# Hybrid encoder layer on one core: the first stage's TensorE order, the places of the next rows' squares, and the turning of the weights' rows

## The chip, the cores and the metric

The kernel runs on one core of one Trainium2 chip. Its engines run side by side and meet through semaphores: PE (TensorE: matrix products and transpositions), DVE (VectorE), ACT (ScalarE), POOL (GpSimd) and SP (SyncE, which here only issues DMAs). The metric is device time in microseconds (us), the median of several runs of the whole kernel.

## The reference, cut to what matters

One encoder layer over 2048 rows of width 1024, all in float32. A conditioning vector c gives six modulation vectors; the rows are normalised, modulated and projected, then go through windowed attention and a bidirectional mLSTM, an output projection, and a gated feed-forward part.

```python
mod = jax.nn.silu(c) @ w_mod + b_mod
shift1, scale1, gate1, shift2, scale2, gate2 = jnp.split(mod, 6, axis=-1)
hmix = rms_norm(x, g_norm1) * (1.0 + scale1) + shift1
q_a, k_a, v_a, q_m, k_m, v_m, o_m, gates = jnp.split(hmix @ w_in, IN_SPLITS, axis=-1)
att = rms_norm(banded_attention(q_a, k_a, v_a, sink), g_attn_out)
qk = jax.nn.silu(centred_dwconv(concat([q_m, k_m]), conv_w, conv_b))
h_m = sigmoid(o_m) * rms_norm(mlstm_forward(qk, v_m, gates) + mlstm_backward(qk, v_m, gates), g_mlstm_out)
x = x + gate1 * (concat([att, h_m]) @ w_out)
hff = rms_norm(x, g_norm2) * (1.0 + scale2) + shift2
gte, up = jnp.split(hff @ w_ffn_in, 2, axis=-1)
x = x + gate2 * ((jax.nn.silu(gte) * up) @ w_ffn_out)
return rms_norm(x, g_final)
```

The edit lies in what makes `hmix` and its first products, and in one store of `o_m`.

## The kernel before, in words

**Tiling.** The rows are 16 tiles of 128 (tt = 0 to 15), in four blocks of 512 (n = 0 to 3). `xts[n]` holds a block's four row tiles, `hT[n]` the normalised and modulated block turned, so that the 1024 columns lie on eight slices k of 128 partitions. Every float32 value goes into TensorE as a high and a low part: `mm3` (L55 to L58) makes a product of three matmuls, high by high, high by low, low by high.

**The first stage** (L282 to L570) does three things side by side. It loads x and the parts of w_mod for the first two modulations, shift (m = 0) and scale (m = 1), in two halves each (`wm`); the first halves come by `mod_sum`, the second ones by `part_sum` on DVE (eight sums over k into `acc[0]` for the scale, into `acc[1]` for the shift), `by_col` (TensorE adds over the partitions and puts the result in columns, bank d), `mod_bias` and `scales` (which makes `gs1`). It normalises: `squares` (ACT, the line of each is L167), `rsqrt` (twelve very small DVE instructions), `scaled`. And it turns the block and multiplies: for slice k `trn(k)` transposes four 128 by 128 pieces on TensorE into PSUM bank b (k even) or d (k odd), `turn(k)` takes them out on ACT with scale and shift (L429) and rounds the high part (L430), `low(k)` makes the low part on DVE (L434), and `prods(k, tiles)` multiplies slice k of some of tiles 0 to 2 by the columns of w_in for values and gates (`nat_mm`: 272 columns into `pa`, 384 into `pv`). Tiles 0 to 2 hold six banks for their sums until slices 6 and 7 are added in the loop below; `nat_hi`, `small_lo` and `nat_lo` split the weights.

**The tile loop** (L525 to L568) goes over blocks and tiles. While block n is multiplied, `norm1(n + 1)` prepares the next one: its first step is squares, rsqrt and scaled; each further step turns one slice (`turned_split`: TensorE L182, ACT L183, DVE L189 and L190). `EVERY` says after how many products a step comes: every second one in tile 3, every eighth in tiles 4 to 7. After a tile its sums are taken out (L559 to L563: `vs` and `va`; `vs` has a single buffer) and stored (L567, L568). `columns_of(1, ...)` turns 48 rows of small weights (norm gains, convolution) into columns with one transposition into bank d and a DVE copy; it stands ahead of tile 4. `mod_row(2)` computes the gate row of the third modulation: loads (L375), sums on DVE (L379, L381), a split (L140, L141), and at the ends of tiles 5 and 6 two matmuls on TensorE (L387, L388).

**Order.** TensorE's order is that of the program in the whole kernel (`hand`). Up to `pre.close()` (L520) the orders of DVE, ACT, POOL and SP are also those of the program. Behind it these engines' instructions are put in order by a planner, by its own reckoning of costs; it may also put later instructions between earlier, fixed ones, as it does with the squares of the second and third block. Every engine and every DMA queue then works in order. The loads and stores of attention (`att_loads`, L842 to L846; the stores L907) go through SP's queue; the stores of `o_tiles` (L652, the gate rows og of the mLSTM heads) go through SP's queue too, but for two that go through ACT's. Their source tile has one buffer.

Of the kernel before, what the change touches and what calls it, by code (L numbers as in the profile page):

```python
# [11 lines left out]
F32 = mybir.dt.float32  # L12
F32R = mybir.dt.float32r
BF16 = mybir.dt.bfloat16
I32 = mybir.dt.int32
AF = mybir.ActivationFunctionType
# [20 lines left out]
def hybrid_layer_kernel(  # L37
# [53 lines left out]
    def rsqrt(pl, v, n, d, tag, bufs=2):  # L91

        vv, hh, yi, a = (pl.tile([P, n], dt, tag=tag + i, name=tag + i, bufs=bufs)
                         for i, dt in (("v", F32), ("h", F32), ("y", I32), ("a", F32)))
        y = yi.bitcast(F32)
        o = 0
        for v_, w, d_ in v if isinstance(v, list) else [(v, n, d)]:
            dve.tensor_scalar(vv[:, o:o + w], v_, 1.0 / d_, EPS, MUL, ADD)
            o += w
        dve.tensor_scalar(yi, vv.bitcast(I32), -0.5, 1597463007.0, MUL, ADD)  # L100
        dve.tensor_scalar(hh, vv, -0.5, None, MUL)
        for _ in range(3):
            dve.tensor_tensor(a, y, y, MUL)
            dve.tensor_tensor(a, a, hh, MUL)
            dve.scalar_tensor_tensor(y, a, 1.5, y, ADD, MUL)
        return y
# [55 lines left out]
    def squares(pl, xt):  # L162

        ssq = pl.tile([P, 4], F32, tag="ssq", name="ssq")
        for i in range(4):
            jk = pl.tile([P, D], BF16, tag="junk", name="junk", bufs=1)
            act.activation(jk, xt[i], AF.Square, accum_out=ssq[:, i:i + 1])  # L167
        return ssq

    def scaled(xt, r, on_act=False):  # L170

        for i in range(4):
            if on_act:
                act.activation(xt[i], xt[i], AF.Copy, scale=r[:, i:i + 1])
            else:
                dve.tensor_scalar(xt[i], xt[i], r[:, i:i + 1], None, MUL)
# [100 lines left out]
    with tc.tile_pool(name="sw", bufs=2, side="right", reuse_waits="tile") as sw:  # L277
# [29 lines left out]
        def columns_of(z, o, n):  # L307
            ps = bank("ad"[z], "colps")
            pe.transpose(ps[:, :n], rows[z], ident[:n, :n])
            dve.tensor_copy(cols[:, o:o + n], ps[:, :n])  # L310
# [32 lines left out]
        def nat_hi(z):  # L343
            act.activation(wh[:, BD[z], :144], wn[z][0], AF.Copy)
            for k in range(4 * z, 4 * z + 4):
                act.activation(wh[:, k, 144:], nat_part(k), AF.Copy)
# [5 lines left out]
        def nat_lo(k):  # L352
            dve.tensor_tensor(wl[:, k, 144:], nat_part(k), wh[:, k, 144:].bitcast(F32), SUB)

        def norm1(n, xt):
            hT.append(Kt(n, f"hT{n}"))
            scaled(xt, rsqrt(s1, squares(s1, xt), 4, D, "rs"))
            yield True
            for k in range(KT):
                turned_split(s1, xt, k, gs1, mod[:, 0, :], hT[n])  # L360
                yield True
# [60 lines left out]
        def trn(k):  # L422
            tps[k] = ps = bank("bd"[k % 2], "trn")
            for i in range(4):
                pe.transpose(ps[:, i * P:(i + 1) * P], x0[i][:, k * P:(k + 1) * P], ident)

        def turn(k):
            t = s1.tile([P, 512], F32, tag="ntmp", name="ntmp", bufs=2)
            act.activation(t, tps.pop(k), AF.Identity, bias=mod[:, 0, k:k + 1], scale=gs1[:, k:k + 1])  # L429
            act.activation(h0(0, k), t, AF.Copy)  # L430
            tps[k] = t

        def low(k):
            dve.tensor_tensor(h0(1, k), tps.pop(k), h0(0, k).bitcast(F32), SUB)  # L434

        def prods(k, tiles):
            for i in tiles:
                deque(nat_mm(0, i, *ops[i], (k,)), 0)

        def part_sum(acc, m, ks):  # L440
            for k in ks:
                w = wm[m, 1][k // 2][:, k % 2, :]
                if k == 0:
                    dve.tensor_scalar(acc, w, sc_col[:, k:k + 1], None, MUL)
                else:
                    dve.scalar_tensor_tensor(acc, w, sc_col[:, k:k + 1], acc, MUL, ADD)

        def by_col(acc):
            ps = bank("d", "modps")
            for k in range(4):  # L450
                pe.matmul(ps[:, k:k + 1], acc[:, k * P:(k + 1) * P], ones[:, 0:1], start=True, stop=True)
            return ps
# [21 lines left out]
        low(0)  # L474
        nat_lo(3)
        trn(2)
        prods(0, range(3))
        turn(1)
        low(1)
        part_sum(acc[0], 1, (0,))  # L480
        trn(3)
        prods(1, range(3))
        turn(2)
        low(2)
        part_sum(acc[0], 1, (1,))
        trn(4)
        prods(2, range(3))
        turn(3)
        low(3)
        part_sum(acc[0], 1, range(2, KT))  # L490
        nat_hi(1)
        ps = by_col(acc[0])
        part_sum(acc[1], 0, range(4))
        mod_bias(1, 1, ps)
# [11 lines left out]
        low(4)  # L506
        prods(4, (0,))
        trn(6)
        turn(5)
        nat_lo(6)  # L510
        low(5)
        prods(4, (1, 2))
        trn(7)
        turn(6)
        nat_lo(7)
        low(6)
        turn(7)
        low(7)
        prods(5, range(3))
        pre.close()  # L520
        gn = cp.tile([P, 2, 2, HM, NT], F32, name="gn")
        bgv = bg.rearrange("p (d y h) -> p y d h", d=2, y=2)
# [2 lines left out]
        for n in range(NB):  # L525
            if n + 1 < NB:
                nrm = norm1(n + 1, xts[n + 1])
                next(nrm)
            if n == 0:
                xts.append(load_x(3))  # L530
            if n == 1:
                vecs = mod_row(2)
                columns_of(1, N_A, N_B)
                dve.tensor_scalar(cvw, cols[:, O_CW:O_CW + 24].rearrange("p (j k) -> p j k", j=3), 0.5, None, MUL)
                dve.tensor_scalar(cvb, cols[:, O_CB:O_CB + KT], 0.5, None, MUL)
                dve.tensor_scalar(gml, cols[:, O_GM:O_GM + HM], 0.5, None, MUL)
            if n + 1 == NB:
                w_first = proj_cols(C_KM)
            for i in range(4):
                tt = 4 * n + i  # L540
                if tt < 3:
                    pa, pv = ops[i]
                else:
                    pa, pv = bank("g", "pa"), bank("a", "pv")
                ev = EVERY[n][i]
                for j, _ in enumerate(nat_mm(n, i, pa, pv, range(6 if tt < 3 else 0, KT))):
                    if ev and j % ev == ev - 1:
                        next(nrm, None)
                if tt == 8:
                    deque(nrm, 0)  # L550
                    wrow = deque(["w1h", "w1l", "wm0", "wm1"])
                    xs.close()
                    wp = ctx.enter_context(tc.tile_pool(name="w", bufs=1, side="left", reuse_waits="tile"))
                    wslots.extend([(wp, 0), (wp, 1)])
                    vecs = chain.from_iterable(mod_row(m) for m in (3, 4))
                vs = sw.tile([P, KV, 2, HD], F32R, tag="vs", name="vs", bufs=1)
                va = sw.tile([P, HM, 129], F32, tag="va", name="va")
                pav = pa[:, :128].rearrange("p (k d) -> p k d", k=KV)
                act.activation(vs[:, :, 0, :], pav, AF.Copy)  # L559
                dve.tensor_tensor(vs[:, :, 1, :], pav, vs[:, :, 0, :].bitcast(F32), SUB)  # L560
                dve.tensor_tensor(gn[:, :, :, :, tt], pa[:, 128:144].rearrange("p (d y h) -> p y d h", d=2, y=2), bgv, ADD)
                act.activation(va[:, 0, :128], pa[:, 144:272], AF.Copy)
                act.activation(va[:, 1:, :128], pv[:, :384].rearrange("p (h d) -> p h d", d=128), AF.Copy)  # L563
                pool.memset(va[:, :, 128:129], 1.0)
                if tt < 9 or tt % 2 == 0:
                    next(vecs, None)
                sp.dma_start(vst_d[tt * P:(tt + 1) * P], vs.bitcast(F32))  # L567
                sp.dma_start(vaug_d[tt * P:(tt + 1) * P], va)  # L568
# [71 lines left out]
    def o_tiles(heads, blocks, ws_):  # L640

        if not ws_:
            ws_.extend(proj_cols(C_OM + h * P) for h in heads)
        for n in blocks:
            for h, w in zip(heads, ws_):
                ps = bank("g", "gps")
                yield from proj_mm(ps, w, n)
                pl, tag = oslots[0]
                oslots.rotate(-1)
                t = pl.tile([P, 512], F32, tag=tag, name="oth", bufs=1)  # L650
                act.activation(t, ps, AF.Tanh, scale=0.5)
                (act if heads == (1,) and n < 2 else sp).dma_start(og_d[n, :, :, h], t.rearrange("p (c t) -> p c t", c=4))  # L652

    later = []

# [1436 lines left out]
```

## Time and profile before

| | |
|---|---|
| runs, median of 3 | 2260.43 us (2260.26 to 2260.79) |
| the profiled execution | 2263.72 us |
| its span, first to last instruction | 2261.9 us |
| mean granted TensorE clock | 0.992 |
| busy: PE, DVE, ACT, POOL | 2216.6 (98%), 1619.1 (72%), 1065.5 (47%), 1035.0 (46%) us |
| chain that ended last | PE 87%, DMA 4%, DVE 4%, ACT 2%, issue 1% |

How to read it: busy times count what an engine executes, not what it waits for. A timeline row gives start, time, engine, line, operation, out<-in, shapes and count, and in brackets the engine's idle time before it with what ended that time. A row of the waits gives who waited for whom, the total, the count and the longest. A row of windows gives the stretch and its length, then for PE, PE's weight loads, DVE, ACT and POOL the busy time with the number of instructions, then the granted clock, the share of the DMA engines and GB/s.

### The profile page before, as it was taken

The page shows a single profiled execution, that of the slowest core. Times are in us where ns is not written, and L with a number is a line of the kernel's source. Part 1 is how long each engine was busy: PE and PEld are TensorE (multiplying, and loading weights), DVE is VectorE, ACT ScalarE, POOL GpSimd, SP SyncE. Part 2 cuts the span into 40 slices and gives each one's busy share as a digit, 9 for nine tenths or more (in the row PEclk, how much of TensorE's full clock was granted, in tenths as well). Part 3 has the DMA queues.
Part 4 walks back from the last instruction along what each step waited for, and adds up shares of the span by engine and source line. Part 5 has one row for each costly group of instructions (what it writes and reads, how often), then busy time and mean ns, then how long its engine had stood idle before and what let it go on. Part 6 is the DMA issues. An engine that isn't in the chain of part 4 may idle for free.

```text
span 2261.9 us, 32339 instructions
## 1 busy us (share of the span) xinstructions
PE 2216.6 (98%) x10808; PEld 1861.0 (82%) x10808; DVE 1619.1 (72%) x2942; ACT 1065.5 (47%) x2216; POOL 1035.0 (46%) x900
## 2 busy tenths in 40 slices
PE   6999999999999999999999999999999999999998
PEld 5998888888788878888888888888888888888887
DVE  6766668656688877886767786777766665785694
ACT  5434565554578746354445434433333333233452
POOL 0016535434343333436666565467665664692020
PEclk8999999999999999999999999999999999999999
DMA  8566755685666575764343454534333374542462
GB/s 311 180 203 218 220 159 173 190 243 162 202 186 188 174 250 205 267 235 156 108 145 110 154 182 168 172 126 140 98 112 98 112 260 141 171 150 95 148 214 93
DMA packets 337063, 391.28 MB, mean 173 GB/s; under 512 B 20874, under 2 KB 234234, under 8 KB 336896
## 3 DMA queue, kind: packets, MB, share of 16 engines
q1 hardware_dynamic: 335616, 388.65, 52.7%
q8 instruction: 85, 1.39, 0.3%
q14 instruction: 82, 0.67, 0.1%
q10 hardware_dynamic: 1280, 0.56, 0.1%
HBM read 269.95 MB, written 119.19 MB: 172 GB/s over the span
## 4 chain that ended last, share of the span: by engine, by line
PE 87%; DMA 4%; DVE 4%; ACT 2%; issue 1%; SPq 0%; POOL 0%; ACTq 0%; POOLq 0%; DVEq 0%
PE gps L579 14%; PE fp L56 12%; PE fp L58 12%; PE fp L57 12%; PE fo L58 5%; PE fo L57 5%; PE fo L56 5%; PE ops L56 2%; PE ops L58 2%; PE ops L57 2%; PE atp L889 1%; PE num L790 1%; PE kvp L703 1%; PE num L792 1%; PE ao L902 1%
## 5 line engine op out<-in xcount | busy, mean ns | idle before, releaser
L579 PE MATMUL gps<-hT,whi 128*128 128x512 f32 x1088 | 395.7, 418 | 1.2 <-DVE cacc L594 1.2
L58 PE MATMUL fo<-w,al 128*128 128x512 f32 x616 | 239.8, 389 | 0.1
L57 PE MATMUL fo<-w,ah 128*128 128x512 f32 x616 | 239.7, 389 | 0.0
L56 PE MATMUL fo<-w,ah 128*128 128x512 f32 x616 | 239.7, 389 | 0.0
L579 PE MATMUL gps<-hT,wlo 128*128 128x512 f32 x544 | 226.3, 416 | 0.0
L579 PEld LDWEIGHTS gps<-hT,whi 128*128 128x128 f32 x1088 | 199.7, 190 | 25.1 <-DVE cacc L594 1.6
L56 PE MATMUL fp<-T,S 128*128 128x512 f32 x528 | 206.7, 391 | 0.0
L57 PE MATMUL fp<-T,S 128*128 128x512 f32 x528 | 205.7, 389 | 0.0
L58 PE MATMUL fp<-T,S 128*128 128x512 f32 x528 | 205.4, 389 | 0.0
L1846 DVE TENSOR_TENSOR al<-al,ah 128x1024 fp32r<-128x1024 f32 x77 | 116.2, 1514 | 105.7 <-ACT ah L1845 105.5
L1845 ACT ACTIVATE ah<-al 128x1024 fp32r<-128x1024 f32 x77 | 81.6, 1060 | 181.9 <-DMA al<-a_d 177.4
L1548 DVE TENSOR_TENSOR S<-sf,S 128x512 fp32r<-128x512 f32 x86 | 130.6, 1556 | 33.4 <-ACT S L1547 33.2
L1548 DVE TENSOR_TENSOR A<-graw,A 128x512 fp32r<-128x512 f32 x86 | 131.4, 1549 | 14.1 <-ACT A L1547 14.1
L58 PE MATMUL fp<-B,A 128*128 128x512 f32 x352 | 136.9, 389 | 0.0
L56 PE MATMUL fp<-B,A 128*128 128x512 f32 x352 | 136.9, 389 | 0.0
L57 PE MATMUL fp<-B,A 128*128 128x512 f32 x352 | 136.9, 389 | 0.0
L58 PEld LDWEIGHTS fo<-w,al 128*128 128x128 f32 x616 | 115.6, 188 | 24.5 <-DVE al L1846 0.6
L56 PEld LDWEIGHTS fo<-w,ah 128*128 128x128 f32 x616 | 115.6, 188 | 24.2
L57 PEld LDWEIGHTS fo<-w,ah 128*128 128x128 f32 x616 | 115.6, 188 | 24.0
L882 POOL TENSOR_SCALAR ap<-ap,adn 128x384 f32<-128x384 f32 (+1 forms) x124 | 70.2, 585 | 134.8 <-PE atp L889 62.3
L1715 DVE SCALAR_TENSOR_TENSOR g<-t,g 128x512 f32<-128x512 f32 x44 | 45.2, 1026 | 114.7 <-ACT t L1714 114.7
L1552 POOL TENSOR_TENSOR sf<-A,A22r 128x512 f32<-128x512 f32 x42 | 58.3, 1389 | 145.5 <-DMA A22r<-in_w_ffn_in_dram 121.7
(448 smaller groups left out, 6157.2 us busy)
## 6 DMA issues: line engine op xcount, KB each, us to landing
al<-a_d SPq DMA_DIRECT2D x77, 512.0 KB, 3.7
wmod<-in_w_mod_dram SPq DMA_DIRECT2D x48, 512.0 KB, 7.6
graw<-in_w_ffn_in_dram SPq DMA_DIRECT2D x43, 512.0 KB, 3.8
a_d<-ka SPq DMA_DIRECT2D x66, 256.0 KB, 4.8
bc<-bc_d SPq DMA_DIRECT2D x64, 256.0 KB, 4.6
hop_d<-n SPq DMA_DIRECT2D x56, 256.0 KB, 3.5
a_d<-u SPq DMA_DIRECT2D x55, 256.0 KB, 4.7
mqk<-qk_d SPq DMA_DIRECT2D x44, 256.0 KB, 4.6
```

Source lines behind the costliest of these rows:

```text
L56: pe.matmul(o, lh, rh, start=first, stop=False, skip_group_check=skip)
L57: pe.matmul(o, lh, rl, start=False, stop=False, skip_group_check=skip)
L58: pe.matmul(o, ll, rh, start=False, stop=last, skip_group_check=skip)
L579: pe.matmul(ps, w[i == 2][:, k, :], hT[n](i == 1, k), start=(k == 0 and i == 0), stop=(k == KT - 1 and i == 2))
L703: pe.matmul(kvp[:, :129], kn, vw, start=True, stop=True)
L790: pe.matmul(num[:, d, :129], sc[:, d, :], va_c, start=True, stop=st is None)
L882: pool.tensor_scalar(p, p, dn[:, g:g + 1], 0.0, MUL, ADD)
L1548: dve.tensor_tensor(t[:, 1, :], f, t[:, 0, :].bitcast(F32), SUB)
L1552: add.tensor_tensor(f1, a21, a22, ADD)
L1715: dve.scalar_tensor_tensor(g0, t0, 1.0, g0, ADD, MUL)
L1845: act.activation(ah, al.bitcast(F32), AF.Copy)
L1846: dve.tensor_tensor(al, al.bitcast(F32), ah.bitcast(F32), SUB)
```

## The change

`squares` is split so that one row tile's square can be placed alone. In the part with fixed orders, trn(3) moves from behind prods(0, tiles 0 to 2) to behind prods(0, tile 0); trn(4) from behind prods(1, tiles 0 to 2) to behind prods(1, tile 0); acc[0]'s third sum moves ahead of the fourth slice's low part. The second block's squares get places on ACT (three behind nat_hi(1), one ahead of turn(5)), its rsqrt and scaled get places on DVE (behind nat_lo(7), which moves ahead of turn(6), and behind low(7)); the third block's squares stand on ACT behind those. `norm1(1)` then has no first step left, and `norm1(2)` only rsqrt and scaled. `columns_of(1, ...)` and the three small scalings behind it move from ahead of tile 4 to ahead of tile 7. In `o_tiles` the two stores through ACT's queue are those of head 0 for blocks 2 and 3, no longer those of head 1 for blocks 0 and 1.

```diff
+    def square(pl, xt, i, ssq):
+        jk = pl.tile([P, D], BF16, tag="junk", name="junk", bufs=1)
+        act.activation(jk, xt[i], AF.Square, accum_out=ssq[:, i:i + 1])
...
         def norm1(n, xt):
             hT.append(Kt(n, f"hT{n}"))
-            scaled(xt, rsqrt(s1, squares(s1, xt), 4, D, "rs"))
+            if n > 1:
+                scaled(xt, rsqrt(s1, ssq2 if n == 2 else squares(s1, xt), 4, D, "rs"))
             yield True
...
         low(0)
         nat_lo(3)
         trn(2)
-        prods(0, range(3))
+        prods(0, (0,))
         turn(1)
         low(1)
         part_sum(acc[0], 1, (0,))
         trn(3)
-        prods(1, range(3))
+        prods(0, (1, 2))
         turn(2)
         low(2)
-        part_sum(acc[0], 1, (1,))
+        part_sum(acc[0], 1, (1, 2))
+        prods(1, (0,))
         trn(4)
-        prods(2, range(3))
+        prods(1, (1, 2))
         turn(3)
         low(3)
-        part_sum(acc[0], 1, range(2, KT))
+        part_sum(acc[0], 1, range(3, KT))
+        prods(2, range(3))
         nat_hi(1)
+        ssq1, ssq2 = (s1.tile([P, 4], F32, tag="ssq", name="ssq") for _ in range(2))
+        for i in range(3):
+            square(s1, xts[1], i, ssq1)
         ps = by_col(acc[0])
...
         trn(6)
+        square(s1, xts[1], 3, ssq1)
         turn(5)
         nat_lo(6)
         low(5)
         prods(4, (1, 2))
         trn(7)
+        nat_lo(7)
+        r1 = rsqrt(s1, ssq1, 4, D, "rs")
         turn(6)
-        nat_lo(7)
         low(6)
         turn(7)
         low(7)
+        scaled(xts[1], r1)
         prods(5, range(3))
+        for i in range(4):
+            square(s1, xts[2], i, ssq2)
         pre.close()
...
             if n == 1:
                 vecs = mod_row(2)
-                columns_of(1, N_A, N_B)
-                dve.tensor_scalar(cvw, cols[:, O_CW:O_CW + 24].rearrange("p (j k) -> p j k", j=3), 0.5, None, MUL)
-                dve.tensor_scalar(cvb, cols[:, O_CB:O_CB + KT], 0.5, None, MUL)
-                dve.tensor_scalar(gml, cols[:, O_GM:O_GM + HM], 0.5, None, MUL)
...
+                if tt == 7:
+                    columns_of(1, N_A, N_B)
+                    dve.tensor_scalar(cvw, cols[:, O_CW:O_CW + 24].rearrange("p (j k) -> p j k", j=3), 0.5, None, MUL)
+                    dve.tensor_scalar(cvb, cols[:, O_CB:O_CB + KT], 0.5, None, MUL)
+                    dve.tensor_scalar(gml, cols[:, O_GM:O_GM + HM], 0.5, None, MUL)
                 for j, _ in enumerate(nat_mm(n, i, pa, pv, range(6 if tt < 3 else 0, KT))):
...
-                (act if heads == (1,) and n < 2 else sp).dma_start(og_d[n, :, :, h], t.rearrange("p (c t) -> p c t", c=4))
+                (act if heads == (0,) and n > 1 else sp).dma_start(og_d[n, :, :, h], t.rearrange("p (c t) -> p c t", c=4))
```

More of the change, by code (lines that the diff above doesn't have):

```diff
@@ L165, in squares @@
         for i in range(4):
-            jk = pl.tile([P, D], BF16, tag="junk", name="junk", bufs=1)
-            act.activation(jk, xt[i], AF.Square, accum_out=ssq[:, i:i + 1])
-        return ssq
+            square(pl, xt, i, ssq)
+        return ssq
+    def square(pl, xt, i, ssq):
+        jk = pl.tile([P, D], BF16, tag="junk", name="junk", bufs=1)
+        act.activation(jk, xt[i], AF.Square, accum_out=ssq[:, i:i + 1])
     def scaled(xt, r, on_act=False):
```

## The prediction, made before the changed kernel was built or run

> **What bounds the kernel now.** I read the page first (PE is busy for 98% of the span and has 87% of the chain that ended last), then the waits of PE, because with PE this full only its own idle time and its clock can give anything back.
>
> ```profile
> PE modps L451 <- DVE macc L446: 4.1, 2, 3.0
> PE colps L309 <- ACT ntmp L183: 3.1, 1, 3.1
> PE as L862 <- DMA ak<-kst_d: 2.2, 1, 2.2
> ```
>
> The first two stand in the stage that is edited, the third in attention, which a store moved by the last hunk touches. Busy time by windows shows what follows such waits: PEclk is the column behind POOL.
>
> ```profile
> 42.30:45.70 3.40, 0.50 (x3) 0.18 (x2) 3.29 (x7) 0.00 (x0) 0.00 (x0) 1.00 1.03 420
> 45.70:49.20 3.50, 3.43 (x14) 3.42 (x15) 2.03 (x5) 1.23 (x2) 0.00 (x0) 0.51 0.57 226
> ...
> 76.50:79.90 3.40, 1.65 (x12) 1.60 (x13) 1.96 (x10) 1.23 (x3) 0.10 (x1) 1.00 0.73 198
> 79.90:83.30 3.40, 3.40 (x17) 3.40 (x16) 2.00 (x5) 0.09 (x1) 0.00 (x0) 0.50 0.84 276
> ```
>
> A stretch in which PE was busy for less than half (0.50 of 3.40, 1.65 of 3.40) is followed by half clock (after the first for two windows: the transposition at 49.26 below still takes 1.05, that at 54.75 takes 0.60), so each wait is paid nearly twice.
>
> **The change, part by part.** All steps are on the trace's own time (span 2261.9, execution 2263.72 us); the runs' median is 2260.43, 3.3 lower, and I take the difference over to it unchanged. Until prods(5) every engine's order is written out by hand, so it can be worked forward.
>
> *1. trn(3) sooner.* PE's, ACT's and DVE's timelines:
>
> ```profile
> 29.21 0.43 PE L56 MATMUL pa<-wnh,hT 128*128 128x272 f32 x1
> ...
> 39.86 1.02 PE L451 MATMUL modps<-ones_r,macc 128*128 128x1 f32 x8 [1.09 <-DVE macc L446]
> ...
> 45.77 1.84 PE L451 MATMUL modps<-ones_r,macc 128*128 128x1 f32 x8 [2.97 <-DVE macc L446]
> ...
> 49.26 1.05 PE L425 MATMUL trn<-ident,xt 128*128 128x128 f32 x4
> ...
> 54.75 0.60 PE L425 MATMUL trn<-ident,xt 128*128 128x128 f32 x4
> ...
> 57.88 0.28 PE L56 MATMUL pa<-wnh,hT 128*128 128x272 f32 x1
> ```
> ```profile
> 32.95 0.78 ACT L429 ACTIVATE ntmp<-trn,mod,gs 128x512 f32<-128x512 f32 x1 [3.21 <-PE trn L425]
> ```
> ```profile
> 29.78 0.69 DVE L434 TENSOR_TENSOR hT<-ntmp,hT 128x512 fp32r<-128x512 f32 x1 [0.24 <-ACT hT L430]
> ...
> 35.04 4.68 DVE L446 SCALAR_TENSOR_TENSOR macc<-wmod,sc_col,macc 128x512 f32<-128x512 f32 x6
> ```
>
> ACT sat idle for 3.21 us until trn(3), which stood behind three tiles of products; low(3) and six of acc[0]'s sums (4.68/6 = 0.78 each) queue behind it on DVE. Now trn(3) comes behind one tile, near 29.3, and takes 1.05 at half clock; ACT has it at 30.3, and 0.78 and the copy's 0.62 end near 31.7. DVE: low(2) until 30.4, two sums until 31.95, low(3) 0.65, five sums 3.9: acc[0] is ready at 36.5 instead of 39.7. PE is the later one then: its products end at 38.77 today (39.86 - 1.09), and a transposition moved into the slow clock adds 0.3: by_col at 39.05 instead of 39.86. On DVE acc[1]'s first four sums end at 39.6, mod_bias waits for by_col until 40.05, four sums of 0.78 end at 43.2. So by_col(acc[1]) goes at 43.35 instead of 45.77: **-2.4**, and PE's wait shrinks from 2.97 to about 1.5. The weights do not hold it: the rows of x loaded right behind them are there at 40.27 (step 3), a load of 512 KB takes 1.25 at 420 GB/s, so acc[1]'s four loads land by 35.3, 36.5, 37.8 and 39.0, and DVE wants them at 36.5, 37.8, 40.1 and 41.6.
>
> *2. The clock.* With a wait of 1.5 PE is busy for over half of any 3.4 us, and I expect full clock. From by_col to tile 0's sixth k took 57.88 - 45.77 = 12.1. At full clock: by_col 0.9, three transpositions and seven tiles of six products 7.5 (one transposition and three tiles take 3.13, 54.75 to 57.88: 0.35 and 0.93 each), and 0.9 for hT's fifth column: PE is there at 45.6, its low part comes at 46.7 (gs at 44.6, then 0.78, 0.62, 0.69). Together 9.3. **-2.7**; bounds 0 (same windows throttled) and -3.6 (no wait for the column). The tile starts at 52.75.
>
> *3. Fixed squares.* They stand on ACT in order, each 1.06 and some 0.15 for the sum's read.
>
> ```profile
> 40.27 1.06 ACT L167 ACTIVATE junk<-xt 128x1024 bf16<-128x1024 f32 x1 [3.21 <-DMA xt<-in_x_dram]
> ...
> 47.98 0.78 ACT L429 ACTIVATE ntmp<-trn,mod,gs 128x512 f32<-128x512 f32 x1 [6.56 <-DVE gs L327]
> 48.65 1.04 ACT L167 ACTIVATE junk<-xt 128x1024 bf16<-128x1024 f32 x1
> ...
> 49.69 0.62 ACT L430 ACTIVATE hT<-ntmp 128x512 fp32r<-128x512 f32 x1
> ```
> ```profile
> 42.99 0.30 SPq L416 DMA_DIRECT2D rows<-in_conv_w_dram  x1
> ```
>
> SP's small loads each wait for an earlier load of x; so the first lands at 40.27, the third at 42.99, and three squares end at 44.2, and turn(4) can start when gs is there, 43.35 + 0.95 + 0.3 = 44.6: hidden, by 0.4. A later landing is paid in full, since turn(4), low(4) and PE's products queue behind. The planner's square now stands between turn(4) and its copy (48.65), so the fixed order loses nothing there. The third block's four squares (4.8 to 5.2) keep ACT from 51.3 until 56.5, ahead of tile 0's copies out of its banks (about 1.0); tile 3 needs those banks at 52.75 + 6 x 0.93 + 0.4 = 58.7: hidden, by 1.2.
>
> *4. r1 on DVE* ahead of low(6) and low(7):
>
> ```profile
> 54.99 0.17 DVE L98 TENSOR_SCALAR rsv<-ssq 128x4 f32<-128x4 f32 x1 [0.98 <-ACT junk L167]
> ...
> 57.66 0.75 DVE L176 TENSOR_SCALAR xt<-xt,rsy 128x1024 f32<-128x1024 f32 x1
> 58.33 0.69 DVE L434 TENSOR_TENSOR hT<-ntmp,hT 128x512 fp32r<-128x512 f32 x1
> ```
>
> Its chain lasts 2.65 (54.99 to 57.66); from 49.85 (square 3 ends at 47.3, turn(5), its copy and low(5) take 2.0, nat_lo(7) 0.6) it ends at 52.5, low(7) at 53.75, where PE wants it at 53.5. PE waits 0.40 for low(7) today, so nothing is added. The next rows are scaled by 56.4 instead of 61.0.
>
> *5. columns_of to tile 7.*
>
> ```profile
> 78.25 0.26 PE L309 MATMUL colps<-ident,rows 48*128 48x48 f32 x1 [3.14 <-ACT ntmp L183]
> 82.92 0.78 PE L182 MATMUL trn<-ident,xt 128*128 128x128 f32 x4
> ```
> ```profile
> 77.25 0.28 ACT L559 ACTIVATE vs<-pa 128x128 fp32r<-128x128 f32 x1 [2.00 <-DMA vst_d<-vs]
> ```
> ```profile
> 66.95 0.42 DVE L189 CAST hT<-ntmp 128x512 fp32r<-128x512 f32 x1
> 67.41 0.69 DVE L190 TENSOR_TENSOR hT<-ntmp,hT 128x512 fp32r<-128x512 f32 x1
> ```
>
> Its transposition takes bank d, which the last transposed column still fills: 3.14, itself 0.2, and tile 4's 24 short products 4.47 (to 82.92) instead of 3.0 (105.30 to 108.31 below), which is the half clock: -4.8. But the column has only moved its due time: tile 4 now wants it 2.7 us after it starts. DVE needs 0.42 + 0.69 a column, 8.9 for eight, and may first do the third block's scaling, until 62.3; with 1.5 for vs and gn it ends at 72.7, which is when PE wants it, and 1.4 later if vs, waiting for its last store, holds ACT as now. I take 0.7: **-4.1**. In its new place columns_of again follows a transposition into bank d, with two products between; at that place now:
>
> ```profile
> 105.09 0.78 ACT L183 ACTIVATE ntmp<-trn,mod,gs 128x512 f32<-128x512 f32 x1
> 105.30 0.29 PE L56 MATMUL pa<-wnh,hT 128*128 128x272 f32 x1
> 108.31 0.60 PE L182 MATMUL trn<-ident,xt 128*128 128x128 f32 x4
> ```
>
> The bank is free at 105.87, PE is there at 105.30: 0.6 and 0.25 for itself, **+0.85**, too short for the clock.
>
> *6. What is late next*: the row of the third modulation, which nobody moves.
>
> ```profile
> 93.75 0.69 DVE L141 TENSOR_TENSOR maccl<-macc,macch 128x512 fp32r<-128x512 f32 x1
> 96.17 0.48 PE L387 MATMUL modrow<-macch,ones_r 128*128 128x512 f32 x1
> ```
>
> PE has 1.7 us of room. Nine us earlier it has it only if the chain of loads and sums comes along; its loads wait for the second block's buffers, free 5 us sooner, and its sums for tile 4's banks, 8 sooner. I charge **+0.5**, between 0 and 7.
>
> *7. The og stores.* Head 0's last two go to ACT's queue, head 1's first two to SP's.
>
> ```profile
> SPq L652 <- ACT ap L868: 2.6, 1, 2.6
> ```
> ```profile
> 592.00:596.00 4.00, 4.00 (x15) 3.42 (x15) 2.54 (x8) 1.90 (x5) 0.00 (x0) 0.59 0.16 49
> ```
> ```profile
> L652 ACTq DMA_DIRECT2D og_d<-oth x2: 521/549/577, 679.8 to 692.8; - x2
> ```
>
> Head 0's third store held SP for 2.6 us at 580 until its Tanh was done, with a load of ak behind it; PE then waited 2.18 for ak, and a stretch at a mean clock of 0.59 followed (4 x 0.41 = 1.6). Without it: 0 to -3.8. In their new places head 1's stores can hold a load in the same way, for as long as their Tanh is late: 0 where that load has 2.6 us of room, else C's price below. On ACT each costs at most its issue, 0.55. Half of it: **-2**, since the planner may put another load or store there. The Trainium skill (Trainium Kernel Development and Optimization, Key Constraints) says that queues share the DMA engines and that issuing from several saves only issue time; by it the term would be about -0.5, but the row shows SP waiting, not issuing.
>
> Sum: -2.4 - 2.7 - 4.1 + 0.85 + 0.5 - 2 = **-9.9**: 2253.8 for an execution like the profiled one, 2250.5 at the median. Behind 120 us PE's waits are few, so what is won early reaches the end.
>
> **Rivals.** *A, the unmoved chain decides* (step 6): if modrow's operands stay at 94.4, PE keeps only its 1.7 us of room: -1.7 + 0.85 - 2 = -2.9, 2257.6. For it: DVE has no room around there.
>
> ```profile
> 83.30:90.00 6.70, 6.70 (x47) 6.67 (x46) 6.47 (x13) 2.40 (x5) 0.14 (x1) 1.00 0.81 267
> ```
>
> Against: its sums wait on tile 4, which comes earlier.
>
> *B, the half clock has another cause* than these waits: 2.7 and the 1.47 of step 5 are not gained, -5.7, 2254.7. Against: both pairs of windows above. The Trainium skill (TensorE: Matmul & The Clock Gate, What's actually happening) speaks for it: it has the gate shut only after a whole idle window of about 3.4 us, and both waits are shorter; by it the time would be B's. The row 76.50:79.90, PE busy for 1.65, contradicts it.
>
> *C, slower*: from pre.close() on DVE, ACT, POOL and SP are put in order by a planner, and another beginning can give another order in attention. One ak load put behind a waiting store costs 2.18, the wait for aptl right after, and 1.6:
>
> ```profile
> 591.13 0.50 PE L902 MATMUL ao<-aptl,av 128*128 128x512 f32 x1 [0.97 <-DVE aptl L141]
> ```
>
> together 4.75. Two new ones eat the first stage's 7.9, and the 2 is not earned: 2262; three: 2267. It decides from the second. Against: PE waited for ak once in 32 units.
>
> *D, the squares do hold ACT*: x lands 2 us later and turn(4) with it: 1.6 and the 2.7 of clock, -5.6, 2254.8.
>
> **How the numbers follow.** Forecast 0.61 (own range 2246 to 2254.5: the stores' whole gain and no late column at the one end, none of the stores' and two us of new waits at the other), A 0.11, B 0.08, C 0.13, D 0.07. A measurement tells 0.2%, 4.5 us, from no change. Faster: the forecast, B, D and 0.02 of A, 0.78; same: the rest of A and C's two loads (0.05), 0.14; slower: C's three, 0.08. The range ends at 2258.5, which takes in A, B and D.
>
> **What would show it.** Right: by_col's second wait near 1.5, clock 1.00 from 43 to 90 us, no wait at columns_of over 1 us, tile 4's first product near 70. Wrong: half clock after 43 us (B), PE waiting at modrow for macc (A), squares ending after gs (D), waits for ak in attention (C).

## The result, and the profile after

| | median (runs) | ratio to before, 95% interval |
|---|---|---|
| before, beside after | 2260.26 us (2258.07 to 2262.58, 7) | |
| after | 2252.69 us (2248.84 to 2254.63, 7) | 0.9966 [0.9954, 0.9978] |
| after once more, with other runs of before beside it (median 2258.67) | 2251.96 us (2250.27 to 2254.76, 7) | 0.9971 [0.9960, 0.9981] |

The change makes the kernel 0.34% faster, 7.6 us at the median; 2250.5 was predicted, 9.9 under the before of that time. The profiled execution of after took 2254.40 us with a span of 2252.6: 9.3 under the span of before. The profiled execution of before (2263.72) is longer than every timed run of before (2255.84 to 2262.58), so 1.7 of the 9.3 come from these two executions, and the medians don't show them. The sum of the forecast is close to the 9.3, its terms are less so.

How far each instruction of PE moved shows where the 9.3 came from. TensorE's instructions are 10808 in both, so the n-th of the one can be set against the n-th of the other where the order is the same:

| instruction of PE | before, us | after, us | moved |
|---|---|---|---|
| first modulation row, L219 (after: L222) | 12.07 | 11.80 | -0.27 |
| by_col(acc[1]) | 45.77 | 42.72 | -3.05 |
| tile 0's sixth slice | 57.88 | 55.32 | -2.56 |
| a product behind low(7) | 59.06 | 55.94 | -3.12 |
| transposition behind tile 4's first 24 products | 82.92 | 76.74 | -6.18 |
| modrow, high part, end of tile 5 | 96.17 | 89.87 | -6.30 |
| first product of tile 7 (behind columns_of in after) | 105.30 | 99.82 | -5.48 |
| a head's product (gps) | 544.11 | 538.29 | -5.82 |
| a head's product after the stores' place | 595.18 | 586.92 | -8.26 |
| a product near 1411 us | 1411.71 | 1402.54 | -9.17 |

First the waits of PE in after, columns: who waited at which line for whom; total, count, longest.

```profile
PE atp L904 <- POOL ap L897: 1.7, 2, 1.4
...
PE modps L455 <- DVE macc L450: 1.5, 1, 1.5
...
PE pa L58 <- DVE hT L193: 0.8, 1, 0.8
...
PE colps L312 <- ACT ntmp L186: 0.5, 1, 0.5
```

The three rows shown of before (modps 4.1 in two, colps 3.1, ak 2.2) have become 1.5 in one, 0.5, and none for ak. In their place stand small ones, for hT's last slice at tile 4 and for `ap` in attention. The timeline of PE in after has them in order of time, with one more for hT behind turn(4):

```profile
42.72 1.02 PE L455 MATMUL modps<-ones_r,macc 128*128 128x1 f32 x8 [1.47 <-DVE macc L450]
...
45.83 0.59 PE L56 MATMUL pa<-wnh,hT 128*128 128x272 f32 x1 [0.64 <-ACT hT L434]
...
71.74 0.37 PE L56 MATMUL pa<-wnh,hT 128*128 128x272 f32 x1
...
75.25 0.39 PE L56 MATMUL pa<-wnh,hT 128*128 128x272 f32 x1 [0.42 <-DVE hT L192]
...
76.51 0.39 PE L58 MATMUL pa<-wnh,hT 128*128 128x272 f32 x1 [0.75 <-DVE hT L193]
76.74 0.60 PE L185 MATMUL trn<-ident,xt 128*128 128x128 f32 x4
...
89.87 0.48 PE L391 MATMUL modrow<-macch,ones_r 128*128 128x512 f32 x1
...
99.64 0.26 PE L312 MATMUL colps<-ident,rows 48*128 48x48 f32 x1 [0.46 <-ACT ntmp L186]
```

by_col(acc[0]) has no wait left, by_col(acc[1]) waits 1.47, and modrow waits for nothing. The windows of after (the clock is the column behind POOL) show the miss:

```profile
42.10:45.50 3.40, 2.47 (x18) 2.23 (x18) 2.51 (x6) 3.29 (x6) 0.00 (x0) 1.00 1.02 418
45.50:48.90 3.40, 3.07 (x11) 2.75 (x12) 2.01 (x4) 2.62 (x5) 0.00 (x0) 0.50 0.61 245
48.90:52.30 3.40, 3.40 (x15) 3.30 (x14) 2.92 (x14) 1.41 (x2) 0.00 (x0) 0.50 0.00 1
...
72.80:76.20 3.40, 2.54 (x17) 1.96 (x15) 3.33 (x10) 1.60 (x4) 0.00 (x0) 1.00 0.68 177
76.20:79.60 3.40, 3.09 (x19) 3.09 (x20) 2.90 (x8) 1.34 (x3) 0.10 (x1) 1.00 1.00 360
```

PE was busy for 2.47 of the 3.40 us ahead of 45.50, and half clock came all the same, for two windows, as before the change (from 45.7 there). The second profile of after has it from 45.7 as well, for one window. Ahead of 76.20 it was busy for about as long, 2.54, and the clock stayed full.

### The profile page after: what moved, and what is told of

Its sections match the earlier page's. It is cut to its first block, busy times and chain, and to the rows that moved or that the text cites. A ratio compares the mean times of both kernels' runs of the same rounds, so it can differ in the third digit from the quotient of the medians.

```text
span 2252.6 us, 32337 instructions
## 1 busy us (share of the span) xinstructions
PE 2214.0 (98%) x10808; PEld 1859.2 (83%) x10808; DVE 1613.5 (72%) x2942; ACT 1067.3 (47%) x2216; POOL 1037.2 (46%) x900
## 4 chain that ended last, share of the span: by engine, by line
PE 69%; ACT 2%; DVE 2%; issue 1%; POOL 0%; DMA 0%; SPq 0%; POOLq 0%; ACTq 0%; DVEq 0%
PE fp L56 12%; PE fp L57 12%; PE fp L58 12%; PE fo L58 6%; PE fo L57 6%; PE fo L56 6%; PE gps L594 3%; PE ops L56 2%; PE ops L58 2%; PE ops L57 2%; PE atp L904 1%; ACT ap L883 1%; PE ao L917 1%; PE as L878 1%; PE as L877 1%
```

## Experiments

Each is the kernel after with one edit (e8: with three), unless it says that it is before with a part of the change. Ratios are to before, run on the same chip. Each has one profile.

| kernel | median, us (range, runs) | ratio, 95% interval |
|---|---|---|
| e1 og stores as before | 2256.08 (2251.6 to 2259.54, 10) | 0.9983 [0.9974, 0.9993] |
| e2 columns_of as before | 2254.81 (2250.97 to 2257.27, 10) | 0.9980 [0.9971, 0.9990] |
| e3 before + PE's order alone | 2257.36 (2254.57 to 2260.34, 10) | 0.9994 [0.9985, 1.0003] |
| e4 before + fixed squares alone | 2259.02 (2256.36 to 2261.7, 10) | 1.0003 [0.9994, 1.0013] |
| e5 filled with products | 2250.67 (2246.59 to 2252.52, 5) | 0.9962 [0.9949, 0.9976] |
| e6 filled with transpositions | 2249.54 (2247.05 to 2250.64, 5) | 0.9959 [0.9947, 0.9972] |
| e7 a third og store on ACT | 2251.32 (2248.99 to 2254.55, 6) | 0.9968 [0.9957, 0.9980] |
| e8 e6, e7 and a later square | 2248.63 (2245.83 to 2251.18, 5) | 0.9957 [0.9944, 0.9971] |
| e9 filled with one-column products | 2250.38 (2248.9 to 2254.53, 5) | 0.9967 [0.9954, 0.9979] |

### The og stores: e1

```diff
-                (act if heads == (0,) and n > 1 else sp).dma_start(og_d[n, :, :, h], ...)
+                (act if heads == (1,) and n < 2 else sp).dma_start(og_d[n, :, :, h], ...)
```

> The changed kernel with the og stores where they were (head 1's first two on ACT's queue, all of head 0's on SP's). Theory (SP's queue stands still until the Tanh is done, with a load of ak behind the store): head 0's third store holds SP for 2 us or more near 574, PE then waits about 2 for ak near 582, and half clock follows; span 2.6 longer than the changed kernel's 2252.6, about 2255. Rival (the move did nothing, the planner's new order made the difference there): no wait for ak, PE's wait of 1.38 for POOL near 579 stays as in the changed kernel, span about 2252.6.

Measured: ratio 0.9983 against 0.9966 and 0.9971 with the new queues, so by the medians the stores' move is worth 0.12 to 0.17%, 2.7 to 3.8 us; the intervals overlap. The Tanh of the third block on ACT in e1, and SP's queue there:

```profile
576.36 0.60 ACT L666 ACTIVATE oth<-gps 128x512 f32<-128x512 f32 x1 [1.83 <-PE as L878]
```

```profile
576.98 0.53 SPq L667 DMA_DIRECT2D og_d<-oth  x1
577.56 0.62 SPq L859 DMA_DIRECT2D ak<-kst_d  x1
```

and SP's queue in after, where ACT issues the third store, and SP the second:

```profile
570.17 0.53 SPq L667 DMA_DIRECT2D og_d<-oth  x1
...
575.06 0.36 SPq L859 DMA_DIRECT2D ak<-kst_d  x1
```

In e1 the store goes when its Tanh is done (576.36 + 0.60), and the load of ak only behind it, at 577.56; in after the load goes 2.5 us sooner. PE's waits at that place, e1:

```profile
578.32 0.44 PE L877 MATMUL as<-ak,aq 128*128 128x384 f32 x1 [1.24 <-DVE nmx L881]
...
582.10 0.41 PE L877 MATMUL as<-ak,aq 128*128 128x384 f32 x1 [0.54 <-DVE adn L891]
...
584.12 0.50 PE L917 MATMUL ao<-aptl,av 128*128 128x512 f32 x1 [0.97 <-DVE aptl L141]
```

2.75 in all. That is less than the theory expected: the longest wait is for DVE's nmx and not for ak, and no half clock follows. In before, e3 and e4, which have the old queues too, PE did wait for ak at this place: 2.18, 0.75 and 1.24. The 0.54 of e1 stands at the same product, and the adn that it is put down to had ended 3.7 us sooner, so it may be that load too; this is not shown. In after there is a new wait of 1.38 for POOL's `ap` and one of 0.38 behind it, 1.76 in all. ACT's timeline in after, with PE's row behind it, says why:

```profile
576.47 0.60 ACT L666 ACTIVATE oth<-gps 128x512 f32<-128x512 f32 x1 [1.74 <-DMA og_d<-oth]
```
```profile
579.48 0.33 PE L904 MATMUL atp<-ident,ap 128*128 128x128 f32 x1 [1.38 <-POOL ap L897]
```

The third Tanh writes the one buffer `oth`, which the second store (SP's, issued at 570.17) had not yet emptied; ACT stood for 1.74, and with it the exponentials that make `ap`.

The length of the place itself, from the head's product at 544 us of the table above to the one behind the stores' place, gives a price without the rest of the kernel:

| | half clock there | us |
|---|---|---|
| old queues: before, e3 | yes | 51.07, 50.20 |
| old queues: e4, e1 | no | 49.48, 48.88 |
| new queues: after, e2 | yes | 48.64, 48.80 |
| new queues: after once more | no | 47.06 |

Like against like, the move is worth 1.4 to 2.4 us there. What the medians of e1 show beyond it is not shown at this place: in its profile e1 loses a further 2.0 against after between 587 and 1404 us, but all save 0.2 of it behind 827 us, past the last moved store. The stretch differs as much between after (815.6) and e2 (817.9), which have the same queues.

### The second store too: e7

```diff
-                (act if heads == (0,) and n > 1 else sp).dma_start(og_d[n, :, :, h], ...)
+                (act if heads == (0,) and n > 0 else sp).dma_start(og_d[n, :, :, h], ...)
```

> The changed kernel with head 0's second og store on ACT's queue as well. Theory (what is left of the wait near 579 is ACT standing at the third Tanh until the second store has landed, a store that SP issued 2.2 late behind its loads): the store goes out near 568, ACT does not wait at the third Tanh (1.74 in the changed kernel), PE's 1.38 and 0.38 near 580 are gone and so is the half clock after: 1.7 to 3.4 less than the changed kernel, ratio to the kernel before about 0.9955. Rival (PE would wait there for the first unit's probabilities anyway): 0 to 0.5 less.

In its trace the Tanh waits for nothing, and PE's two waits are one of 0.45:

```profile
573.27 0.58 ACT L666 ACTIVATE oth<-gps 128x512 f32<-128x512 f32 x1
```
```profile
577.19 1.18 PE L904 MATMUL atp<-ident,ap 128*128 128x128 f32 x4 [0.45 <-POOL ap L897]
```

So the wait is explained, and the place took 45.95 us, 1.1 less than the 47.06 of after once more. The 1.7 to 3.4 that the theory expected did not come: the median is 0.6 under after's on the same chip, and the ratio, 0.9968, cannot be told from that of after.

### columns_of: e2

```diff
             if n == 1:
                 vecs = mod_row(2)
+                columns_of(1, N_A, N_B)
...
-                if tt == 7:
-                    columns_of(1, N_A, N_B)
```

(the three small scalings move with it)

> The changed kernel with columns_of back ahead of tile 4. Theory (the wait for bank d is a wait of its own and drags the clock down): PE waits 2.5 to 3.1 at columns_of, the next 3.4 us run at half clock, no wait at tile 7 and none for the eighth column in tile 4 (0.42 and 0.75 in the changed kernel): span 2.5 to 3.5 longer than 2252.6. Rival (tile 4 waits for the same eighth column anyway, so the wait only changes its name): span 0.5 longer at most.

```profile
74.53 0.26 PE L312 MATMUL colps<-ident,rows 48*128 48x48 f32 x1 [2.78 <-ACT ntmp L186]
```
```profile
72.40:75.80 3.40, 1.27 (x9) 1.22 (x10) 3.33 (x14) 1.74 (x4) 0.00 (x0) 0.99 0.61 160
75.80:79.20 3.40, 3.40 (x17) 3.40 (x16) 2.50 (x6) 0.00 (x0) 0.11 (x1) 0.50 0.97 348
```

With the old place the old wait and the half clock behind it are back, and the waits for the eighth column are gone. The ratio, 0.9980 against 0.9966 and 0.9971, puts both places of the move together at 0.09 to 0.14%, 2.0 to 3.2 us; the intervals overlap here too. The traces of e3 and e4 (next section), which have the old place as well, show what that gain hangs on: there columns_of waits 1.92 and 2.91, and the clock stays full.

```profile
75.79 0.26 PE L312 MATMUL colps<-ident,rows 48*128 48x48 f32 x1 [2.91 <-ACT ntmp L186]
```
```profile
71.30:74.70 3.40, 1.58 (x11) 1.30 (x10) 1.90 (x8) 1.38 (x4) 0.21 (x2) 1.00 0.22 81
74.70:78.10 3.40, 2.31 (x18) 2.26 (x19) 3.33 (x13) 0.94 (x2) 0.00 (x0) 1.00 0.87 257
```

(both of e4). From the product behind low(7) to tile 7's first product the old place takes 46.24 (before) and 45.84 (e2) with the half clock, 43.55 (e3) and 44.53 (e4) without it; the new place takes 43.7 to 43.9 in the profiles of after, e1 and e7. (e3 and e4 also lack one half of the new order, so the comparison is not of this edit alone.) So the wait by itself was mostly exchanged for the wait for the eighth column, as the rival had it, and what the move gains, 2.0 to 2.5, is the half clock in those executions in which it comes.

### The two halves of the hand-written order: e3 and e4

e3 is before with the moves of trn, prods and part_sum alone, e4 is before with `square`, the fixed squares, `rsqrt` and `scaled` alone; the lines are those of the diff above.

> The kernel before with TensorE's new order and the third sum moved, nothing else. Theory (the late trn(3) alone made the two waits at by_col): the first wait is gone, the second about 1.5, by_col(acc[1]) near 43.0 instead of 45.77; half clock still follows from about 45.5 on, so PE reaches tile 0's sixth slice about 2.8 sooner and keeps the 3.1 at columns_of: span about 2259. Rival (the squares' fixed places are needed for it): less than 1 us at by_col, span about 2261.5.

> The kernel before with the squares, rsqrt and scaling of the second and third block at their fixed places, nothing else. Theory (they only hold places that the planner had filled as well): waits at by_col as before, 1.1 and 3.0; wait at columns_of between 2.5 and 3.1; span within 1 us of 2261.9. Rival (they carry part of the gain, by giving the eighth column of the second block sooner): the wait at columns_of under 1.5 and no half clock behind it, span near 2259.

Neither median can be told from before: -1.4 us in proportion for e3 (0.06%), +0.7 for e4. The profiles' spans are 2255.1 in both, where both theories expected more (2259 and near 2261.9); with such medians that says more of the profile of before, which has a half-clock window behind columns_of that neither of them has. In e3's trace the wait of by_col(acc[1]) shrinks as predicted, and most of that comes back right behind it, as a wait for turn(4)'s copy, which the planner puts a square ahead of:

```profile
42.52 1.02 PE L451 MATMUL modps<-ones_r,macc 128*128 128x1 f32 x8 [1.46 <-DVE macc L446]
...
46.29 0.60 PE L56 MATMUL pa<-wnh,hT 128*128 128x272 f32 x1 [1.31 <-ACT hT L430]
```

In after, with both halves, this second wait is 0.64. e4 alone leaves by_col's waits in place (1.10 and 2.04). The four parts by their ratios (stores 0.14, columns_of 0.11, order 0.06, squares -0.03) add up to 0.28%, where after measures 0.29 and 0.34; but each part is about as small as half the width of its interval (0.1%), so the sum fits and proves little.

### What the clock follows: e5, e6 and e9

In after PE is busy for 73% of the window ahead of 45.50, and half clock follows. Three kernels fill by_col(acc[1])'s wait of 1.47 with work of which nothing is used, each of another kind:

```diff
-        def by_col(acc):
+        def by_col(acc, more=0):
             ps = bank("d", "modps")
+            for _ in range(more):
+                pe.matmul(ps[:, 128:512], h0(0, 2, slice(0, P)), wh[:, 2, NA:NA + NV], start=True, stop=True)  # e5, more=7
+                pe.transpose(ps[:, 128:256], x0[0][:, 0:P], ident)  # e6, more=15
+                pe.matmul(ps[:, 128:129], x0[0][:, 0:P], ones[:, 0:1], start=True, stop=True)  # e9, more=6
```

(one of the three lines in each)

> The changed kernel with seven products of 384 columns more on TensorE ahead of by_col(acc[1]), into columns of its bank that nobody reads; they take about 1.2 of the wait of 1.47. Theory (half clock from 45.5 on follows from too few products in the window before, and one-column products and transpositions hardly count): full clock from 32 to 60, tile 0's sixth slice about 3 us sooner than in the changed kernel, 2 to 3 us less at the end, ratio to the kernel before 0.9955. Rival (idle time under 1.5 is not what sets the clock): half clock as before, the same time or 0.2 more.

> The changed kernel with fifteen transpositions of 128 columns at the same place, about as long (1.3) and read by nobody. Theory (transpositions hardly count for the clock): PE is busy for over 85% of the window, and half clock follows all the same; time as the changed kernel or 0.3 more. Rival (any busy time counts): full clock from 32 to 60 as with the products, 2 to 3 us less.

> The kernel after with 6 one-column products (12 records of 0.114 us, 1.4 us) ahead of by_col(acc[1]) in place of e6's 15 transpositions: PE is as busy in the wait by the profile, but with products of one column. T (one-column products do not count for the clock, which is why windows with by_col in them were followed by half clock at 73% busy): half clock for one or two windows of 3.4 us behind the wait, between 44 and 53 us, as in after, and the median at after's, 2252 to 2253. Rival (any busy time counts): full clock from 30 us to past 800 as in e5 and e6, the median 2249.5 to 2250.7.

With products of 384 columns the clock is full from 32 to 813 us, with transpositions from 29 to 814, but for one window at 186.3 behind a wait of 2.81 for `cacc`. That transpositions hardly count, the theory of e6, fell. e9 then filled the wait as fully, with products of one column: its PE timeline, the windows of e9, and for comparison one of e6:

```profile
40.06 1.39 PE L455 MATMUL modps<-ones_r,xt 128*128 128x1 f32 x12
42.08 1.05 PE L457 MATMUL modps<-ones_r,macc 128*128 128x1 f32 x8 [0.62 <-DVE macc L450]
```
```profile
39.80:43.20 3.40, 2.77 (x24) 2.69 (x23) 3.33 (x5) 3.02 (x5) 0.00 (x0) 1.00 1.02 418
43.20:46.60 3.40, 3.40 (x15) 3.31 (x15) 2.13 (x6) 3.37 (x7) 0.00 (x0) 0.50 1.03 423
```
```profile
42.90:46.30 3.40, 2.21 (x14) 1.71 (x14) 1.89 (x6) 3.37 (x7) 0.00 (x0) 1.00 1.03 422
```

In e9 PE is busy for 2.77 of the window ahead of 43.20, more than in e6's window ahead of 46.30 (2.21), and yet half clock follows in e9 and not in e6. Of the 2.77, 2.44 are products of one column. So such products count for little in what sets the clock, though the profile shows PE busy in them, and the forecast's busy share was the wrong measure. e9's median (2250.38) lies within the range of the theory that fell (2249.5 to 2250.7, where the other had 2252 to 2253); the trace decides, in one execution. What exactly is counted, and the share from which the clock falls, stay open: e4's window 71.30:74.70 was busy for 1.58 without any one-column products, and full clock followed, while 1.65 without any was followed by half clock (76.50:79.90, in the prediction).

Why e9 is no slower for its half clock, its trace says too. From by_col(acc[1]) to tile 0's sixth slice it took 10.18, e5 10.06 and e6 10.36: at full clock PE only comes sooner to turn(4)'s copy and waits for it (0.70 in e5, 0.98 in e6, nothing in e9). And all three gained something that has nothing to do with the clock: with the unused products in the kernel the planner put ACT's work behind 59 us in another order. It takes the seventh slice ahead of `vs`, where after takes `vs` first and waits 1.66 for its store (shown under step 5). Here e6; e5 and e9 have the same order:

```profile
67.38 0.78 ACT L186 ACTIVATE ntmp<-trn,mod,gs 128x512 f32<-128x512 f32 x1 [0.29 <-PE trn L185]
68.06 0.27 ACT L576 ACTIVATE vs<-pa 128x128 fp32r<-128x128 f32 x1
```

In e5, e6 and e9 tile 4 waits for no column, and the stretch from the product behind low(7) to tile 7's first product takes 42.0 to 42.1, against 43.9 and 43.7 in the two profiles of after. So about 1.7 of what these three are ahead of after at tile 7 comes with the planner's other order.

### All together: e8

```diff
-        for i in range(3):
+        for i in range(2):
             square(s1, xts[1], i, ssq1)
...
         turn(4)
+        square(s1, xts[1], 2, ssq1)
```

with e6's transpositions and e7's store.

> The kernel after with three edits at once: the 15 transpositions ahead of by_col(acc[1]) (e6), the third of the next rows' squares put behind turn(4) instead of ahead of it, and head 0's second og store on ACT too (e7). T (the gains add): full clock from 30 us to past 800, turn(4)'s first step starts when gs is ready, near 43.4 instead of 43.8, PE's wait for hT after it 0.6 instead of 0.98, near 577 one wait of about 0.5 instead of 1.3 + 0.4; the median is 1 us under e6's 2249.5, ratio to before 0.9955. Rival (what is won early is given back): DVE's rows of gates near 180 us do not come sooner, PE waits 2.5 to 3.2 for cacc near 186 as in e6 (2.81), with half clock behind it, and the median stays within 1 us of e6's, 0.996 or above.

turn(4) now starts when gs is ready, and PE's wait for it is 0.44 instead of e6's 0.98:

```profile
43.29 0.78 ACT L433 ACTIVATE ntmp<-trn,mod,gs 128x512 f32<-128x512 f32 x1 [0.86 <-DVE gs L330]
```
```profile
44.78 0.39 PE L56 MATMUL pa<-wnh,hT 128*128 128x272 f32 x1 [0.44 <-ACT hT L434]
```

The wait near 574 is 0.46, the clock full from 30 to 812 us, and the wait for `cacc` near 185, 2.81 in e6, is 1.08 here: the rival's giving back did not show. The planner's order is another one again (tile 4 waits 0.33 for its eighth column). The median, 2248.63, is the lowest of all kernels here, but 0.9 under e6 is less than these runs can tell. It beats before by 0.43%; against after (0.9966, 0.9971) the intervals overlap.

## Why the prediction was right, by its steps

That the total came out is partly luck: the misses cancel, and the profile of before that it was reckoned from was a long one. By the table of PE's instructions, each step against what was put for it:

| step | put | measured, between the instructions of |
|---|---|---|
| 1 trn(3) sooner | -2.4 | -3.05, to by_col(acc[1]) |
| 2 clock | -2.7 | +0.49, to tile 0's sixth slice |
| 3, 4 squares, r1 | 0 | -0.56, to behind low(7) |
| 5 columns_of, old place | -4.1 | -3.06, to behind tile 4's first products |
| 6 modrow | +0.5 | -0.12, to modrow |
| 5 columns_of, new place | +0.85 | +0.82, to tile 7 |
| none | 0 | -0.34, to 544 us |
| 7 og stores | -2 | -2.44, to 595 us |
| none | 0 | -0.91, to 1411 us |
| sum | -9.85 | -9.17 |

**Step 1** was right, in mechanism and size: by_col(acc[1])'s wait is 1.47 where 1.5 was put, and 0.27 of the 3.05 came in with the first loads.

**Step 2** is the one that failed: +0.49 in this execution, half a us beyond the bound of 0 ("same windows throttled"), and -1.05 in the second profile of after (42.73 to 53.79), where one window was at half clock. The prediction's own sign for that, half clock after 43 us, came in both. The sentence that failed is "PE is busy for over half of any 3.4 us, and I expect full clock": PE was busy for 73%, and the clock fell. e9 shows for one execution that one-column products, the 1.02 of by_col in that window, hardly count. Rival B, a cause other than these waits, is not right for that: filling the wait (e5, e6) kept the clock full. The +0.49 is mostly the wait of 0.64 for hT. The size was too large as well: with the clock full, e5 and e6 took 10.06 and 10.36 for the stretch that was put at 9.3, so the term would have been -1.8 to -2.0 and not -2.7. Around turn(4) PE lost more there than the 0.9 that was put, in part by step 3: e8, with the third square out of turn(4)'s way, took 9.70.

**Step 3** (squares hidden by 0.4) came out 0.3 short. ACT and then DVE in after:

```profile
43.30 1.06 ACT L171 ACTIVATE junk<-xt 128x1024 bf16<-128x1024 f32 x1
44.35 0.76 ACT L433 ACTIVATE ntmp<-trn,mod,gs 128x512 f32<-128x512 f32 x1
```
```profile
43.86 0.15 DVE L330 SCALAR_TENSOR_TENSOR gs<-mod,cols 128x4 f32<-128x4 f32 x1
```

gs is there at 44.01, 0.6 sooner than put, and the third square ends at 44.36 instead of 44.2; turn(4) starts right behind it, at 44.35: D in miniature. **Step 4** (r1 on DVE, nothing) added no wait; the one of 0.40 for low(7) went.

**Step 5.** The wait and the half clock went, as put; e3 and e4 show that the half clock does not follow such a wait in every execution, and that without it the move gains 0.7 or nothing. The eighth column was mis-sized: 0.7 was charged, within 0 to 1.4, and tile 4's 24 short products took 5.0 (71.74 to 76.74) instead of the 3.0 of undisturbed ones: 2.0, of which 0.42 + 0.75 stand as waits. That vs, waiting for its last store, would hold ACT was the upper bound's reason, and it did:

```profile
72.12 0.28 ACT L574 ACTIVATE vs<-pa 128x128 fp32r<-128x128 f32 x1 [1.66 <-DMA vst_d<-vs]
```

**Step 6** cost nothing: maccl's row on DVE in after ends at 88.65, and PE, at 89.87, had 1.2 of room, where it had 1.7 before. The chain came along, and A fell.

```profile
87.96 0.69 DVE L141 TENSOR_TENSOR maccl<-macc,macch 128x512 fp32r<-128x512 f32 x1
```

**Step 7** was right in mechanism, and near in size: -2.44 between the two profiles, 1.4 to 2.4 like against like (e1), where half of the bound of 3.8 was taken. The -0.91 behind it is not the stores': 0.7 of it arises near 836 us, behind a stretch of half clock that both kernels have. The rule of the Trainium skill (Trainium Kernel Development and Optimization, Key Constraints), that another issuer saves issue time alone, put 0.5; the trace shows more, and what saved it is that a store waits for its producer at the head of an in-order queue, ahead of a load. The half clock at 592 us went, though one at 581.4 to 584.8 took its place in the profiled execution; the second profile of after, with nearly the same wait there (1.26), has none. C did not occur: PE never waits for ak in after.

## What to carry to other kernels

Move a store out of a queue with loads on PE's path where its producer is late; and look next at the store that frees the source buffer, since a single buffer ties it to the next producer. A transposition into a shared bank costs its wait for the bank's last reader, and in some executions the half clock after it, so put it where PE reaches that bank late, and check that the wait does not come back under another name. Where PE waits next to one-column products, don't count these as busy when you ask whether the clock will hold; unused products or transpositions in the wait kept it (e5, e6), with medians 1.3 and 2.4 us under after's on the same chip, which the intervals don't separate from after, and part of which is the planner's order. Where a planner orders the other engines, compare their order before a difference is put down to the edit.

## What the runs showed of the hardware

The clock's half-speed stretches came in multiples of 3.41 us (3.41, 6.83, 10.24; the last one of each execution ends with it), and at other times from one execution to the next. In the first 90 us they were, in the traces: before 21.9 to 32.1, 45.7 to 52.6, 79.9 to 83.3; after 21.6 to 31.8, 45.5 to 52.3; after again 21.8 to 32.1, 45.7 to 49.1; e5 21.4 to 31.6 alone, e6 22.5 to 29.3 alone. The kernel after thus had two windows in one profile and one in the other, behind nearly equal windows (busy 2.47 and 2.54); e1, e2 and e7, which begin alike, had two, two and one. And behind columns_of half clock came after waits of 3.14 and 2.78 (before, e2), not after 1.92 and 2.91 (e3, e4). That may be what spreads the runs of one kernel over 4.5 to 5.8 us; it was not shown, since of each kernel one execution is profiled (of after two).

The Trainium skill (TensorE: Matmul & The Clock Gate, What's actually happening) says that the clock is watched in free-running windows of about 3.4 us, so that where an edge falls varies from run to run: the lengths and the two profiles of after agree. It also has the gate go down after an idle window; here it went down after windows that were busy for 1.65, 2.47 and 2.77 of 3.40 us by the profile, and there the measurement decides.
